# A decoder layer's output projection in seven block products, with its weight sums on GpSimd and their low parts through DRAM

## The chip, the core and the metric

The kernel runs on one core of one Trainium2 chip. The metric is device time in microseconds (us) of one execution: 1641.2 us before the change, the median of 3 runs (1641.06 to 1641.68). A core has a matrix engine (PE, whose weight loads are shown as PEld), a vector engine (DVE), an activation engine (ACT), GpSimd (POOL) and SyncE (SP), which here only issues DMAs. Each engine takes its own instructions strictly in order; they wait for one another through semaphores.

## The reference, cut to what matters

```python
merged = (gates[:, :, 0] * (y_sb @ w_sb_out[l])
          + gates[:, :, 1] * (y_ml @ w_ml_out[l])
          + gates[:, :, 2] * (y_xa @ w_xa_out[l]))
x = x + merged @ w_o[l]

h = _rmsnorm(x, g_ffn[l])
u = _causal_dwconv(h @ w_up[l], ff_conv_w[l], ff_conv_b[l])
```

The sequence has 1024 rows and the model 1024 columns, all in float32. Three mixers (stick-breaking attention, mLSTM, cross-attention) make y_sb, y_ml and y_xa of 512 columns each. Their projections are gated and added (`merged`), and one 1024 x 1024 product with `w_o` writes to the residual stream. An RMS norm and a gated MLP follow.

## The kernel before

Everything lies transposed, columns on the 128 partitions and the 1024 sequence rows along the free axis, in tiles of 128 x 1024 floats (a page, 512 KB). h = 1 and h = 0 name the two halves of 512 rows. To keep float32 precision PE multiplies in three passes: each operand is split into a rounded part `hi` and a rest `lo` (`split`, L128: a copy on ACT at L129, a subtraction on DVE at L130), and `mm3` (L141) does hi by hi, hi by lo, lo by hi, three matmuls of 128 x 512 (L142 to L144) for one block of 128 x 128 weights. In PSUM there are eight banks of 128 x 512: two each under the tags pj, pv, tr and z.

Three stages matter here.

**The branch stage** (L1067 to L1088). For each of three branches b and each of eight column blocks n, PE makes two banks (h = 1, 0) of four `mm3`, 24 matmuls in all, from the branch's weights `w_br` and the split pages `ys` of y. DVE takes each bank with the gate (`scalar_tensor_tensor`, L1083 and L1085) and adds it to `merged[n]` (L1086). The gates, the weights and the y pages come from DRAM by SP: gates through tag U (L1057), weights through `raw` (L135), the four y pages of branches 1 and 2 through `px` (L1064, two buffers), from where they are split into `h`. The y pages of branch 0 are split into `pg`. So b = 2 needs four pages through the two `px` buffers.

**The output projection** (L1091 to L1149). `merged` is split into `m_hi` and `m_lo`, half by half, beside the end of the branch stage. Then for h = 1 and h = 0 and each of eight column blocks d, `proj` loads and splits a page of `w_o` and runs eight `mm3`: 2 x 8 x 8 x 3 = 384 matmuls. `ev` (L1114) takes the bank into the residual x1 (L1119), stores x1 to DRAM (L1120), and squares and adds it for the norm (L1123 to L1126). During h = 0 the norm of h = 1 is applied and the first MLP operands are made (`h2_upper`, L1100), and `diff` is begun (L1130).

**The MLP's entry** (L1176 to L1211). The MLP already works by seven block products in place of eight (`seven`, L694, Winograd's form of Strassen). Its operands need sums of the four quarters of the normed x1, made and split on DVE and ACT from L1188 on while PE begins the first products.

The order on each engine is made by a scheduler when the kernel is built, by priorities and by its own guess of durations; on the chip it is fixed. A tile pool gives out a tag's buffers in turn: who wants a buffer waits until its last user is done.

## Time and profile before

| | before |
|---|---|
| median of 3 runs | 1641.2 us |
| the profiled execution | 1641.45 us |
| its span, first to last instruction | 1639.7 us |
| PE busy, share of the span | 99% |
| DVE, ACT, POOL busy | 74%, 50%, 6% |
| granted TensorE clock | 1.000 |
| DMA, mean over the span | 130 GB/s |

The span is 1.75 us shorter than the profiled execution's time. A row of a timeline gives start (us from the span's start), duration, engine, line, operation, output and inputs, and in brackets how long the engine had been idle and who ended that. Matmuls overlap, so a matmul's duration of 0.39 us is longer than the distance from one to the next. A group of a source view gives durations in ns as least, median and greatest.

### The profile page before, as it was taken

Reading aid. Unit: us, or ns where it says so; the run is one execution under the profiler, and the core shown is the slowest. Engines: PE = TensorE matmul, PEld = TensorE weight load, DVE = VectorE, ACT = ScalarE, POOL = GpSimd, SP = SyncE. Lnnn points to the kernel's source line nnn. Section 1 sums busy time; section 2 is a strip of 40 time slices with the busy share of each in tenths; the row PEclk is TensorE's granted clock in tenths of the full one; section 3 lists DMA queues with packets and bytes.
Section 4 is the critical chain, followed back from the end, with each engine's and each line's share of the span. In section 5 each row is a group of like instructions: output and inputs, shape, how many; then the busy total and the mean of one; then the engine's idle time right before and its main releaser. Section 6 shows DMA issues by size and latency. Waiting matters only on the chain.

```text
span 1639.7 us, 21300 instructions
## 1 busy us (share of the span) xinstructions
PE 1623.8 (99%) x8007; PEld 1330.6 (81%) x8007; DVE 1205.9 (74%) x1672; ACT 822.3 (50%) x1269; POOL 95.9 (6%) x164
## 2 busy tenths in 40 slices
PE   8999999999999999999999999999999999999999
PEld 4878888888888888888888888788888888888887
DVE  5658888759764776776657658997777777799764
ACT  4557777545554444666412334655555545543431
POOL 1022222020000010100000000000000000000000
PEclk9999999999999999999999999999999999999999
DMA  8420111324324665434844453322222221576131
GB/s 298 155 66 21 39 40 65 140 94 152 129 99 154 191 193 156 137 115 153 313 151 129 155 187 107 123 97 71 78 78 100 92 78 52 177 310 244 46 135 71
DMA packets 97426, 212.70 MB, mean 130 GB/s; under 512 B 13416, under 2 KB 37288, under 8 KB 97324
## 3 DMA queue, kind: packets, MB, share of 16 engines
q1 hardware_dynamic: 97324, 211.35, 38.1%
q8 instruction: 63, 1.03, 0.3%
q14 instruction: 39, 0.32, 0.1%
HBM read 156.71 MB, written 54.61 MB: 129 GB/s over the span
## 4 chain that ended last, share of the span: by engine, by line
PE 93%; DVE 3%; DMA 2%; ACT 1%; issue 1%; SPq 0%; POOLq 0%; POOL 0%; ACTq 0%; DVEq 0%
PE ps_pj L142 15%; PE ps_pj L143 15%; PE ps_pj L144 15%; PE ps_pv L142 6%; PE ps_pv L144 6%; PE ps_pv L143 6%; PE ps_tr L144 4%; PE ps_tr L142 4%; PE ps_tr L143 4%; PE ps_z L142 3%; PE ps_z L143 3%; PE ps_z L144 3%; PE ps_pv L444 2%; PE ps_tr L424 2%; PE ps_z L399 1%; PE ps_z L398 1%
## 5 line engine op out<-in xcount | busy, mean ns | idle before, releaser
L143 PE MATMUL ps_pj<-h,whi 128*128 128x512 f32 x624 | 244.1, 391 | 1.0 <-DVE h L130 1.0
L129 ACT ACTIVATE whi<-raw 128x512 fp32r<-128x512 f32 (+1 forms) x111 | 93.1, 839 | 180.8 <-PE ps_pj L143 74.8
L142 PE MATMUL ps_pj<-h,whi 128*128 128x512 f32 x416 | 165.9, 399 | 0.2 <-ACT h L129 0.2
L142 PE MATMUL ps_pj<-pg,whi 128*128 128x512 f32 x396 | 154.4, 390 | 0.0
L144 PE MATMUL ps_pj<-pg,wlo 128*128 128x512 f32 x376 | 146.5, 390 | 0.0
L143 PEld LDWEIGHTS ps_pj<-h,whi 128*128 128x128 f32 x624 | 117.3, 188 | 25.1 <-DVE h L130 1.9
L144 PE MATMUL ps_pj<-h,wlo 128*128 128x512 f32 x328 | 128.2, 391 | 0.1
L835 DVE SCALAR_TENSOR_TENSOR y<-U,vec,y 128x1023 f32<-128x1023 f32 x88 | 112.4, 1278 | 7.6 <-ACT y L833 7.5
L412 DVE TENSOR_TENSOR_SCAN U<-U 128x512 f32<-128x512 f32 (+3 forms) x96 | 92.7, 1007 | 22.1 <-POOL U L407 20.5
L142 PEld LDWEIGHTS ps_pj<-h,whi 128*128 128x128 f32 x416 | 78.2, 188 | 16.3 <-ACT h L129 1.1
L142 PEld LDWEIGHTS ps_pj<-pg,whi 128*128 128x128 f32 x396 | 74.3, 188 | 15.2
L144 PEld LDWEIGHTS ps_pj<-pg,wlo 128*128 128x128 f32 x376 | 70.6, 188 | 15.0 <-DVE wlo L130 0.3
L130 DVE TENSOR_TENSOR wlo<-raw,whi 128x1024 fp32r<-128x1024 f32 x54 | 65.9, 1221 | 18.3 <-ACT whi L129 18.3
L143 PE MATMUL ps_pj<-pg,whi 128*128 128x512 f32 x188 | 73.4, 390 | 0.0
L144 PEld LDWEIGHTS ps_pj<-h,wlo 128*128 128x128 f32 x328 | 61.6, 188 | 13.8 <-DVE wlo L130 0.6
L129 ACT ACTIVATE whi<-pg 128x512 fp32r<-128x512 f32 (+1 forms) x46 | 35.3, 769 | 61.8 <-PE ps_pv L143 18.2
L833 ACT ACTIVATE y<-U,vec 128x1024 f32<-128x1024 f32 x44 | 54.6, 1241 | 17.4 <-DVE U L726 16.9
L144 PE MATMUL ps_pj<-h,whi 128*128 128x512 f32 x160 | 62.3, 390 | 0.0
L144 PE MATMUL ps_pv<-pg,wlo 128*128 128x512 f32 x150 | 58.4, 389 | 0.0
L130 DVE TENSOR_TENSOR wlo<-raw,wlo 128x512 fp32r<-128x512 f32 x55 | 37.8, 687 | 26.5 <-ACT wlo L129 26.2
L401 ACT ACTIVATE U<-ps_z 128x1024 f32<-128x1024 f32 (+3 forms) x48 | 39.1, 814 | 31.9 <-PE ps_z L399 24.0
L144 PE MATMUL ps_tr<-pg,wlo 128*128 128x512 f32 x140 | 54.5, 389 | 0.0
(463 smaller groups left out, 4310.4 us busy)
## 6 DMA issues: line engine op xcount, KB each, us to landing
raw<-in_w_t_dram SPq DMA_DIRECT2D x29, 512.0 KB
gate_d<-U SPq DMA_DIRECT2D x24, 512.0 KB
U<-gate_d SPq DMA_DIRECT2D x22, 512.0 KB
act_d<-y SPq DMA_DIRECT2D x22, 512.0 KB
pg<-in_w_t_dram SPq DMA_DIRECT2D x21, 512.0 KB
raw<-in_w_dn_dram SPq DMA_DIRECT2D x18, 512.0 KB
raw<-in_w_o_dram SPq DMA_DIRECT2D x16, 512.0 KB
h<-act_d SPq DMA_DIRECT2D x14, 512.0 KB
```

The costliest lines, as they stand in the source:

```text
L129: nc.scalar.activation(hi, src, AF.Copy)
L130: (eng or nc.vector).tensor_sub(lo, src, hi.bitcast(F32))
L142: nc.tensor.matmul(out, lh, rh, start=start, stop=False, skip_group_check=more)
L143: nc.tensor.matmul(out, lh, rl, start=False, stop=False, skip_group_check=more)
L144: nc.tensor.matmul(out, ll, rh, start=False, stop=stop, skip_group_check=more)
L398: nc.tensor.matmul(z[:, a, :w], qs[a][:, ts(rb)], ks[a][:, c], start=True, stop=False)
L401: nc.scalar.activation(f[:, :, 1:w + 1], z[:, :, :w], AF.Sigmoid, scale=-0.125)
L412: nc.vector.tensor_tensor_scan(f[:, a, 1:w + 1], f[:, a, 1:w + 1], f[:, a, 1:w + 1], 1.0 if o == 0 else f[:, a, 0:1], op0=ALU.mult, op1=AL ...
L424: nc.tensor.transpose(pt[:, a, ts(j)], g[:, a, ts(j)], ident)
L444: nc.tensor.matmul(pv[64 * a:64 * a + 64, ts(rb % 4)], sbv[s // 2][:, s % 2, (2 * p + a) * 64:(2 * p + a + 1) * 64], wt[a][:, ts(j)], star ...
L833: nc.scalar.activation(out, u, AF.Identity, bias=bias, scale=taps[0])
L835: nc.vector.scalar_tensor_tensor(out[:, :S - s], u[:, s:], taps[s], out[:, :S - s], op0=ALU.mult, op1=ALU.add)
```

## The change

It concerns the three stages above. `merged` now lies as quarters (two halves of the rows, two halves of the columns), and the output projection becomes seven block products, each of 4 column blocks by 4 inner blocks by 3 passes = 48 matmuls: 336 in place of 384. The seven products accumulate in two sets of four banks (L: pj and tr, R: pv and z). Three of them use plain quarters of `w_o`, loaded and split as before (`raw_w`). The other four use sums of quarters, S1 to S4, each of two pages. GpSimd makes these sums in the branch stage (`wo_sums`, one step of the generator behind each unit of branches 1 and 2), eight additions and subtractions of 128 x 1024. For each of the eight sum pages `spill` also makes the rounded part (on ACT) and the rest (on GpSimd), both in the two `px` buffers, and SP stores the rest to DRAM (`slo_d`). In the projection `sum_w` rounds the sum page again on ACT and fetches the rest from DRAM by a DMA that GpSimd issues.

In the branch stage the column blocks come in the order 0, 4, 1, 5, ... and each `w_br` load brings two blocks that lie apart. The x1 quarters are built up in place from the loaded x (`grow`): 32 reads of a bank by DVE in place of 16. The MLP's upper operands are made two blocks at a time (`upper`).

```diff
+    ORDER = (0, 4, 1, 5, 2, 6, 3, 7)
+    merged = [[[page() for _ in range(2)] for _ in range(2)] for _ in range(2)]
+    slo_d = dtile([4, 2, P, S], "slo_d")
...
+    def wo_load(q, i, j, tag):
+        t = T([P, S], tag)
+        n = 4 * i + 2 * j
+        nc.sync.dma_start(t.rearrange("p (n c) -> p n c", n=2), w_o[n:n + 2, :, hs(q)].rearrange("n p c -> p n c"))
+        return t
...
+    def spill(i, j):
+        hi, lo = T([P, S], "px", F32R), T([P, S], "px", F32R)
+        split(ws[i][j], hi, lo, nc.gpsimd)
+        nc.sync.dma_start(slo_d[i, j], lo.bitcast(F32))
+
+    def wo_sums(j):
+        a1, a2 = wo_load(0, 0, j, "pg"), wo_load(0, 1, j, "pg")
+        yield
+        nc.gpsimd.tensor_sub(a2, a1, a2)
+        ws[2][j] = a2
+        spill(2, j)
+        b2 = wo_load(1, 1, j, "pg")
+        yield
+        nc.gpsimd.tensor_sub(b2, b2, a2)
+        ws[1][j] = b2
+        spill(1, j)
...
     for i in range(3 * KT):
-        b, n = i // KT, i % KT
+        b, n = i // KT, ORDER[i % KT]
         if n == 0:
             ys = [branch(b, j) for j in range(4)]
...
+        if b:
+            next(beside, None)
+        if i == 3 * KT - 5:
+            first_operands(0)
+        if i >= 3 * KT - 2:
+            w1.append(wsplit(None, raw=wo_load(0, 0, len(w1), "raw")))
...
+    def part_product(banks, w, n, start):
+        for d in range(4):
+            hi, lo = w[d // 2]
+            for k in range(4):
+                c = slice((4 * (d % 2) + k) * P, (4 * (d % 2) + k + 1) * P)
+                mh, ml = m[n][k // 2]
+                mm3(banks[d], hi[:, c], lo[:, c], mh[:, hs(k % 2)], ml[:, hs(k % 2)], start and k == 0, k == 3, not start)
+            yield d
...
+    def sum_w(i, j):
+        t = [T([P, S], tag, F32R) for tag in ("whi", "wlo")]
+        nc.scalar.activation(t[0], ws[i][j], AF.Copy)
+        nc.gpsimd.dma_start(t[1], slo_d[i, j])
+        return t
...
+    for d in part_product(L, w6, "t1", False):
+        if d == 0:
+            r = rstd(acc[1], HALF, "z")
...
+        if d > 1:
+            upper(0, o1u, d - 2, dau)
+        grow(o2l, L, d)
+        squares(0, part(o2l, d))
+        if d % 2:
+            keep(o2l, 1, 0, d // 2)
+        grow(o1l, L, d)
...
+    for d in part_product(R, w7, "bl", True):
...
+        grow(o1l, R, d)
+        squares(0, part(o1l, d))
+        nc.vector.scalar_tensor_tensor(part(diff, d), part(o1l, d), minus[:, d:d + 1], part(o2l, d), op0=ALU.mult,
+                                       op1=ALU.add)
+        if d % 2:
+            keep(o1l, 0, 0, d // 2)
+            upper(2, o2u, d // 2, dbu)
```

Three places show what the scheduler made of it. The first is SP's queue in the branch stage. Before, the loads of branch 2's four y pages (px from y_d) stand among the gate (U) and weight (raw) loads of the start of branch 1:

```order
L1064 DMA px_7681<-y_d 128x1024
L1057 DMA U_7345<-gate_d 128x1024
L135 DMA raw_7471<-in_w_br_dram 128x1024
L1064 DMA px_7687<-y_d 128x1024
L1057 DMA U_7375<-gate_d 128x1024
L1064 DMA px_7693<-y_d 128x1024
L1064 DMA px_7699<-y_d 128x1024
L1057 DMA U_7437<-gate_d 128x1024
```

In the changed kernel the same four loads, px_7746 to px_7764, stand behind the stores of all eight rests (slo_d); the last of these stores are:

```order
L1079 DMA slo_d<-px_7696 128x1024
L1125 DMA raw_7840<-in_w_br_dram 128x2x512
L1058 DMA U_7806<-gate_d 128x1024
L1079 DMA slo_d<-px_7736 128x1024
L1125 DMA raw_7916<-in_w_br_dram 128x2x512
L1058 DMA U_7838<-gate_d 128x1024
L1079 DMA slo_d<-px_7742 128x1024
L1065 DMA px_7746<-y_d 128x1024
L1065 DMA px_7752<-y_d 128x1024
L1058 DMA U_7876<-gate_d 128x1024
L1125 DMA raw_7986<-in_w_br_dram 128x2x512
L1065 DMA px_7758<-y_d 128x1024
```

The y pages of branch 2 moved from the start of branch 1 to behind the eighth store, and each store waits for GpSimd's subtraction that makes it; gate and weight loads stand between the stores.

The second place is GpSimd's queue behind the mixers. Before, its last instructions are small ones, the reciprocal roots of the norms (L150):

```order
L150 TENSOR_TENSOR sm_5895<-sm_5893,nhalf 128x8
L150 TENSOR_TENSOR sm_6220<-sm_6218,nhalf 128x8
L150 TENSOR_TENSOR sm_6537<-sm_6535,nhalf 128x8
L150 TENSOR_TENSOR sm_6847<-sm_6845,nhalf 128x8
L150 TENSOR_TENSOR sm_8430<-sm_8428,nhalf 128x4
```

Now sixteen operations of 128 x 1024 stand there, of which the first twelve are these (pg are weight pages and their sums; L130 with px is the subtraction that makes a rest):

```order
L1084 TENSOR_TENSOR pg_7442<-pg_7440,pg_7442 128x1024
L1089 TENSOR_TENSOR pg_7482<-pg_7482,pg_7442 128x1024
L130 TENSOR_TENSOR px_7478<-pg_7442,px_7477 128x1024
L1094 TENSOR_TENSOR pg_7440<-pg_7440,pg_7482 128x1024
L1097 TENSOR_TENSOR pg_7528<-pg_7528,pg_7482 128x1024
L130 TENSOR_TENSOR px_7524<-pg_7482,px_7523 128x1024
L1084 TENSOR_TENSOR pg_7614<-pg_7612,pg_7614 128x1024
L130 TENSOR_TENSOR px_7564<-pg_7440,px_7563 128x1024
L1089 TENSOR_TENSOR pg_7654<-pg_7654,pg_7614 128x1024
L1094 TENSOR_TENSOR pg_7612<-pg_7612,pg_7654 128x1024
L130 TENSOR_TENSOR px_7570<-pg_7528,px_7569 128x1024
L130 TENSOR_TENSOR px_7650<-pg_7614,px_7649 128x1024
```

Nothing is moved here; it is added. Two sums stand ahead of the first rest, two more ahead of the second, one ahead of the third, two ahead of the fourth; of the last four rests (the fifth is the last row) only the sixth has a sum ahead of it.

The third place is DVE's queue at the end of the projection. Before, for the column blocks d = 4 to 6 of h = 0 (L1119 takes a bank, L130 splits a weight page or an operand):

```order
L1102 SCALAR_TENSOR_TENSOR pg_8032<-U_8047,vec,ps_tr_8437 128x512 x2
L1102 SCALAR_TENSOR_TENSOR pg_8033<-U_8048,vec,ps_tr_8437 128x512
L1119 SCALAR_TENSOR_TENSOR px_8347<-ps_pj_8541,hf_8566 128x512
L1102 SCALAR_TENSOR_TENSOR pg_8033<-U_8048,vec,ps_tr_8437 128x512
L1130 SCALAR_TENSOR_TENSOR h_8042<-px_8347,vec,y_8345 128x512
L1126 TENSOR_TENSOR hf_8344<-hf_8344,hf_8566 128x512
L130 TENSOR_TENSOR h_8038<-pg_8032,h_8038 128x512
L130 TENSOR_TENSOR wlo_8624<-raw_8621,whi_8623 128x1024
L1119 SCALAR_TENSOR_TENSOR px_8347<-ps_pj_8583,hf_8608 128x512
L1130 SCALAR_TENSOR_TENSOR h_8042<-px_8347,vec,y_8345 128x512
```

Now, for the last part (L1186 takes a bank, L1268 makes two blocks of an upper operand, L1202 adds squares):

```order
L1202 TENSOR_TENSOR hf_8071<-hf_8071,hf_8606 128x512
L1186 SCALAR_TENSOR_TENSOR y_8491<-ps_pv_8611,y_8491 128x512
L1268 TENSOR_TENSOR pg_8489<-U_8315,raw_8558 128x1024
L1308 SCALAR_TENSOR_TENSOR h_8495<-y_8491,sm_8505,px_8173 128x512
L1186 SCALAR_TENSOR_TENSOR y_8491<-ps_pv_8612,y_8491 128x512
L1202 TENSOR_TENSOR hf_8071<-hf_8071,hf_8643 128x512
L1308 SCALAR_TENSOR_TENSOR h_8495<-y_8491,sm_8505,px_8173 128x512
L130 TENSOR_TENSOR h_8502<-pg_8489,h_8501 128x1024
L1202 TENSOR_TENSOR hf_8071<-hf_8071,hf_8660 128x512
L130 TENSOR_TENSOR U_8680<-me_8631,U_8680 128x512
```

The split of a weight page has gone from this stretch, and more reads of banks and the operands' multiplications and splits of 128 x 1024 have come into it, while a column block now lasts 12 matmuls where it lasted 24.

More of the change, by code (lines that the diff above doesn't have):

```diff
@@ new lines, in both, with gain, operand @@
+    def both(op, t, rows):
+        v = t.rearrange("p (k r) -> p k r", k=2)
+        op(v, v, rows.unsqueeze(1).to_broadcast([P, 2, HALF]))
+    def gain(o, i):
+        for d in range(4):
+            nc.scalar.activation(part(o, d), part(o, d), AF.Copy, scale=col(C_GFFN + 4 * i + d))
+    L, R = four(LONG[::-1]), four(SHORT)
+    w2, w3, w4, w5, w6, w7 = ([None, None] for _ in range(6))
+    def operand(n, src):
+        for j in range(2):
+            m[n][j] = fine(src[j], "h")
+    o1u = out_tiles(0, 1, "U")
@@ new lines, in tile_hybrid_layer @@
+    operand("bu", bu)
+    operand("t3", al)
+    for d in part_product(L, w1, "au", True):
+        if d % 2 == 0:
+            w2[d // 2] = raw_w(1, 0, d // 2)
+        grow(o1u, L, d)
+    operand("t2", au)
+    o2l = out_tiles(1, 0, "px")
+    for d in part_product(R, w2, "bu", True):
+        if d % 2 == 0:
+            w3[d // 2] = sum_w(2, d // 2)
+        grow(o1u, R, d)
+    for j in range(2):
+        keep(o1u, 0, 1, j)
+        nc.vector.tensor_sub(bu[j], bu[j], au[j])
+    R = four(SHORT)
@@ L1153, in tile_hybrid_layer @@
+    x1p = o1l + o2l
     act_d = dtile([NF // 2, 2, P, S], "act_d")
@@ L1189, in tile_hybrid_layer @@
         for j in range(2):
-            for i in range(2):
-                nc.vector.tensor_mul(diff[j][:, hs(i)], diff[j][:, hs(i)], rows)
+            both(nc.vector.tensor_mul, diff[j], rows)
             nc.vector.tensor_add(full[j], full[j], diff[j])
```

180 lines of the change are left out of this document (115 added, 65 removed).

## The prediction

> **What bounds the kernel now.** I read the page first: which engine is busy all the time.
>
> ```profile
> span 1639.7 us, 21300 instructions
> PE 1623.8 (99%) x8007; PEld 1330.6 (81%) x8007; DVE 1205.9 (74%) x1672; ACT 822.3 (50%) x1269; POOL 95.9 (6%) x164
> ```
>
> PE is. Then the table of stages (busy us and instructions per engine, clock, DMA share, GB/s), cut at the starts of the branches, the projection and the MLP's entry, and PE's own waits between 783 and 1050 us (us in total, times, longest).
>
> ```profile
> 826.70:870.20 43.50, 43.50 (x193) 36.03 (x192) 26.01 (x35) 4.24 (x4) 0.00 (x0) 1.00 0.47 145
> 870.20:913.80 43.60, 43.60 (x194) 36.08 (x194) 34.58 (x50) 13.64 (x20) 0.00 (x0) 1.00 0.33 104
> 913.80:1001.50 87.70, 87.70 (x391) 72.40 (x390) 54.55 (x76) 33.30 (x46) 1.89 (x1) 1.00 0.58 190
> 1001.50:1050.00 48.50, 47.31 (x207) 37.55 (x206) 46.50 (x65) 25.77 (x38) 1.01 (x1) 1.00 0.20 68
> ```
>
> ```profile
> PE ps_pj L143 <- DVE h L130: 1.0, 2, 0.5
> PE ps_pj L142 <- ACT h L129: 0.2, 1, 0.2
> ```
>
> In branch 1 (826.7 to 870.2), branch 2 (to 913.8) and the projection (to 1001.5) PE never waits. At the entry it waits 1.2 us, and DVE is nearly as full as PE: 46.5 of 48.5 us. So a matmul less is time saved, as long as nothing new makes PE wait. GpSimd stands idle in branches 1 and 2.
>
> **Part 1, the matmuls.** Two rows of PE's timeline that stand 48 matmuls apart:
>
> ```profile
> 791.36 0.39 PE L142 MATMUL ps_pj<-pg,whi 128*128 128x512 f32 x1
> ...
> 802.24 0.39 PE L142 MATMUL ps_pj<-pg,whi 128*128 128x512 f32 x1
> ```
>
> 48 matmuls take 10.88 us, 0.227 us each. The projection goes from 384 to 336, so **-10.9 us**. That is the whole gain.
>
> **Part 2, the spills.** Branch 2 can't start before its first y page is loaded (px) and rounded. By the order of SP that load now stands behind the stores of all eight rests, and a rest needs the px buffer that the store before it has to empty. So there is a chain: store of one rest, GpSimd's subtraction for the next, its store, eight times over. I need its start, the store S and a GpSimd operation P.
>
> The start: the weight pages for the sums take the pg buffers of branch 0's y pages, free in its last bank.
>
> ```profile
> 826.49 0.39 PE L144 MATMUL ps_pj<-pg,wlo 128*128 128x512 f32 x1
> 826.72 0.39 PE L142 MATMUL ps_pj<-h,whi 128*128 128x512 f32 x1
> ```
>
> Branch 0's last matmul starts at 826.5, branch 1's first at 826.7, and branch 2's by 192 matmuls more at 870.2. A bank is 12 matmuls, 2.7 us, and its first three read the first pages, so these loads go out at about 825. For a page's way from DRAM I take SP's issues of px pages and ACT's start on them:
>
> ```profile
> 799.91 0.33 SPq L1064 DMA_DIRECT2D px<-y_d  x1
> 805.63 0.32 SPq L1064 DMA_DIRECT2D px<-y_d  x1
> 808.99 0.32 SPq L1064 DMA_DIRECT2D px<-y_d  x1
> ```
>
> ```profile
> 803.28 1.06 ACT L129 ACTIVATE h<-px 128x1024 fp32r<-128x1024 f32 x1 [3.46 <-DMA px<-y_d]
> 809.25 1.06 ACT L129 ACTIVATE h<-px 128x1024 fp32r<-128x1024 f32 x1 [1.54 <-DMA px<-y_d]
> 814.22 1.06 ACT L129 ACTIVATE h<-px 128x1024 fp32r<-128x1024 f32 x1 [3.91 <-DMA px<-y_d]
> ```
>
> 3.4 and 3.6 us, and 5.2 where others are under way. The first sum needs two pages, one behind the other: 825 + 5 = 830. A store of a whole page isn't in these rows; as the same bytes in the other direction I take S = 3.6, with 3.4 and 5.2 as ends.
>
> P has no row either. The nearest, in ns (least, median, greatest):
>
> ```profile
> L498 POOL TENSOR_TENSOR mw<-mw,mw x1: 453/453/453, 94.0 to 94.0; 32x128 f32<-32x128 f32 x1
> L880 POOL TENSOR_SCALAR_AFFINE_SELECT me<-me x8: 634/739/1079, 357.9 to 626.2; 128x512 f32<-128x512 f32 x8
> L407 POOL TENSOR_SCALAR_AFFINE_SELECT U<-U x64: 398/408/1387, 103.2 to 298.0; 128x256 f32<-128x256 f32 x64
> ```
>
> One input: 634 - 398 = 236 ns for 256 columns, so 0.92 a column over a fixed 0.16 us, and 1.1 us for 1024: the lower end. Two inputs: 453 ns for 128 columns; less 0.16 that is 2.3 ns a column, 2.5 us for 1024; scaled whole it is 3.6, the upper end. I take P = 2.3, a little under 2.5, since two inputs may well cost more of the fixed part. The Trainium skill, "GPSIMD Engine Reference", section "Elementwise — side-by-side cycle accounting", gives 4497 ns for a two-input addition of 2048 floats on GpSimd against 2293 on DVE; half of that, 2.25 us, is an estimate from that page, and by it the sum would be 0.7 us less. The same page's "Engine selection" speaks against this change: elementwise work belongs on VectorE.
>
> Now the chain, by GpSimd's order. Two sums and a rest: 3P = 6.9, so 836.9. Of the seven cycles that follow, two have two sums inside (4.6, more than S): 3P = 6.9 each. The other five are S + P = 5.9 each. 836.9 + 13.8 + 29.5 = 880.2.
>
> To this comes the meeting of DVE and GpSimd:
>
> ```profile
> 162.25 1.22 DVE L130 TENSOR_TENSOR wlo<-raw,whi 128x1024 fp32r<-128x1024 f32 x1
> ...
> 162.49 1.60 POOL L407 TENSOR_SCALAR_AFFINE_SELECT U<-U 128x256 f32<-128x256 f32 x2
> ```
>
> Two GpSimd operations beside a DVE subtraction of two SBUF tiles took 1.60 us together, where two medians are 0.82: 0.8 lost to one meeting. In branch 1 DVE has 16 additions of 0.69 and four splits of 1.22 of that kind, 16 of 43.5 us; about a third of the 14 operations on the chain meet one, at half of it on average (0.4): +2 us, 882.2. (The rule for this is a rival, below.)
>
> Then SP stores and issues the y page (0.35), it lands (3.6), ACT rounds it (1.06): 887.2 in place of 870.2, **+17.0 us**.
>
> **Part 3, the other y pages.** Before, they were loaded during branch 1. Now page 1 waits for the eighth store, 882.2 + 3.6 = 885.8, lands at 889.4, is rounded at 890.5, and its rest is made at 891.7:
>
> ```profile
> L130 DVE TENSOR_TENSOR h<-px,h x8: 1216/1224/1226, 798.7 to 821.4; 128x1024 fp32r<-128x1024 f32 x8
> ```
>
> Only then is its buffer free for page 3: 891.7 + 3.6 + 1.06 + 1.22 = 897.6. The first bank of branch 2 needs page 3's rest for its last two matmuls, so it ends at 898.1, against 887.2 + 2.7 = 889.9: **+8.2 us**. While PE waits in either part, DVE falls idle; there is no cover to lose. Queued behind the waiting stores on SP are gate and weight loads, and behind ACT's roundings for the spills, which wait for GpSimd's sums, ACT's roundings of the weight pages. DVE waits for both and PE for DVE; but the chain doesn't depend on them, so they only make PE wait earlier for part of what it would wait for at branch 2.
>
> **Part 4, the projection itself.** The rests come back by GpSimd's own DMAs, which the profile before doesn't show. A weight page serves 24 matmuls, 5.4 us, and there are two buffers, so a load that takes under 5.4 us (the rows above have 3.4 to 5.2) is hidden: 0, up to +1 for each of eight loads if it takes 6.4. The Trainium skill, "DMA: Bandwidth & Descriptors", section "Anatomy of one DMA — SWDGE (gpsimd) path", would put it at 2.0 us plus bytes over 436 GB/s, an estimate of 3.2 us for a page; by that too the term is 0. The splits of `merged` were hidden beside the branch stage and are, as seven operands, spread over the parts (DVE has 33 us free there); the first of them are made before part 1. `rstd` stands behind the first bank of part 6 and needs the last squares of part 5, some 2 us of ACT and DVE behind a bank of 2.7 us with ACT's weight rounding in between: **+1 us**.
>
> **Part 5, DVE at the end.** DVE's work in the last two parts against the same stretch before:
>
> ```profile
> 979.70:1001.50 21.80, 21.80 (x98) 18.05 (x97) 18.29 (x27) 9.64 (x15) 0.00 (x0) 1.00 0.65 205
> ```
>
> ```profile
> L1119 DVE SCALAR_TENSOR_TENSOR U<-ps_pj,hf x8: 690/690/693, 919.4 to 957.5; 128x512 f32<-128x512 f32 x8
> L1126 DVE TENSOR_TENSOR hf<-hf,hf x14: 682/684/687, 926.9 to 1004.7; 128x512 f32<-128x512 f32 x14
> L1130 DVE SCALAR_TENSOR_TENSOR h<-px,vec,y x4: 743/749/753, 987.7 to 1004.0; 128x512 f32<-128x512 f32 x4
> L170 DVE TENSOR_SCALAR hf<-ident,sm x8: 277/279/285, 971.4 to 1008.6; 128x128 f32<-128x128 f32 x8
> ```
>
> Now 12 reads of banks (8.3), 7 additions of squares (4.8), four upper operands multiplied and split (8 x 1.22 = 9.8), four `diff` (3.0), four 128 x 128 (1.1) and two half splits (1.4): 28.4 us in two parts of 10.9, 21.8. 6.6 us pass on to the entry, where DVE has 2.0 free. Fewer, longer operations there save 0.5, and waits among these operations eat about as much: **+5 us**, from 0 to 8.
>
> **Sum**: -10.9 + 17.0 + 8.2 + 1 + 5 = +20.3. The profiled execution, 1641.45 with 1.75 outside its span, would become 1661.8; it lies 0.25 over the median of 1641.2, so I predict **1661.5 us**.
>
> **The rivals.**
>
> *GpSimd is quick* (P = 1.1, the one-input pace). Every cycle is then S + P = 4.7: 830 + 3.3 + 32.9 = 866.2, plus 1 for meetings and 5.0 for the page: 872.2, +2.0. The sum is -10.9 + 2.0 + 8.2 + 1 + 5 = +5.3, 1646.5 us. Against it: the two-input row is twice the one-input slope.
>
> *GpSimd is slow, or the rests come back late.* With P = 2.9, between 2.5 and the upper end, part 2 grows by 14 x 0.6 = 8.4: 1670. With 3.6 by 18: 1680. Loads of 6.4 us add 8.
>
> *DVE and GpSimd shut each other out.* If each holds the other off for a whole instruction, GpSimd's 16 x 2.3 = 36.8 us and DVE's two-input work of 16 to 20 us share the 57 us from 830 to 887 and just fill them. A few cycles then wait for a whole DVE operation: some 3 to 5 us in place of my 2, 1664. The Trainium skill, "SBUF — State Buffer", section "Who interferes with whom", states just this: a DVE instruction with two SBUF inputs and a GpSimd instruction that reads SBUF exclude each other. The 1.60 us row agrees.
>
> *Hidden (the other side).* The spills stay ahead of branch 2, so neither part 2 nor 3 is paid: -10.9 + 1 + 5 = -4.9, 1636.5 us. It decides where the last rest is made 13 us before 870.2, at 857: 27 us for eight rests, 3.4 each. With S alone at 3.4 GpSimd would have to take nothing. For it speaks only that a store may land sooner than a load.
>
> *It does not do what it says*: the count of matmuls in the program falls by 48, so this is out.
>
> **How the numbers follow.** Forecast with its near bounds, 1654 to 1670: 0.52. DVE and GpSimd shutting each other out, 1660 to 1670: 0.12. GpSimd slow or late rests, above 1670: 0.16. GpSimd quick, 1645 to 1654: 0.12. Hidden or nearly so: 0.08, of which 0.05 below 1638 and 0.03 about the old time. A measurement of this kernel can tell about 0.2%, 3.3 us, from no change. The range of 8 in 10 takes in the quick and some of the slow case: 1645 to 1677. Faster 0.05, same 0.03, slower 0.92.
>
> **What would show it.** Right: PE waits between 826 and 900, in two lumps, one in branch 1 behind a bank that DVE can't take (it waits for a late weight page), one at branch 2's start behind ACT's rounding of px, 25 us together; GpSimd's L130 rows about 2.3 us each, 6 us apart; the table of stages with DVE full at the entry and PE idle 6 us there. Wrong: GpSimd's 128 x 1024 operations near 1.1 us; branch 2 starting less than 5 us behind branch 1's last matmul; stores that land in under 3 us; PE waits inside the seven parts for `wlo`.

## The result, and the profile after

The changed kernel takes 1669.4 us (median of 4 runs, 1666.3 to 1670.6) against 1641.2 before, a ratio of 1.0168 with a 95% interval of 1.0151 to 1.0186: slower by 28.2 us, where 20.3 were forecast (the time lies inside the range of 1645 to 1677). The profiled execution took 1668.9, with a span of 1667.2. Its page:

```profile
span 1667.2 us, 21227 instructions
PE 1627.1 (98%) x7959; PEld 1326.9 (80%) x7959; DVE 1234.3 (74%) x1673; ACT 838.5 (50%) x1278; POOL 140.7 (8%) x188
```

The 48 matmuls are gone (8007 to 7959), and yet PE is busy 3.3 us longer. So not only waits were added. The table of stages, cut at the first matmul of branch 1, branch 2, the projection and what follows its 336 matmuls, shows why (the columns are those of before):

```profile
825.67:889.51 63.84, 46.87 (x193) 37.16 (x191) 44.49 (x39) 14.48 (x14) 41.34 (x16) 0.90 0.72 243
889.51:939.42 49.91, 48.93 (x193) 37.12 (x193) 34.52 (x43) 9.42 (x9) 0.00 (x0) 0.92 0.52 162
939.42:1020.91 81.49, 79.84 (x347) 65.40 (x346) 62.02 (x81) 44.99 (x57) 5.62 (x9) 0.98 0.43 130
1020.91:1069.40 48.49, 42.60 (x168) 32.50 (x167) 45.22 (x60) 22.47 (x32) 1.42 (x1) 0.93 0.22 73
```

Branch 1 takes 63.8 us (the wait for branch 2's first page counted in) and branch 2 49.9, where each took 43.5, and the granted clock, 1.00 in each stage before, is below 1 in all four. PE's waits from 826 to 1050 us:

```profile
PE ps_pj L142 <- DVE U L1138: 11.7, 3, 10.3
PE ps_pj L142 <- ACT h L129: 7.5, 4, 5.6
PE ps_z L158 <- DVE hf L1202: 1.6, 1, 1.6
PE ps_pj L144 <- DVE U L130: 1.5, 1, 1.5
PE ps_pj L143 <- DVE h L130: 1.3, 1, 1.3
PE ps_tr L158 <- DVE hf L1202: 0.6, 1, 0.6
PE ps_pv L143 <- DVE h L130: 0.4, 1, 0.4
```

They are the two lumps that were forecast, 10.3 us in branch 1 behind a bank and 5.6 at branch 2's start behind ACT's rounding of a y page, and then small ones at `rstd` and the entry. But the lumps were to make 25 us together. In the two branches PE is idle for 17.0 and 1.0 us (length less busy in the table); the other 8.8 of the 26.7 us lost there are busy time, 3.4 and 5.4 more than the 43.5 of before. What the forecast lacks is half clock: windows like these three, behind the branches (length, PE busy and its instructions, ..., the clock before the last two columns):

```profile
999.65:1003.06 3.41, 3.41 (x10) 2.65 (x9) 1.42 (x5) 1.33 (x2) 1.04 (x1) 0.50 0.01 3
1030.37:1033.78 3.41, 3.41 (x10) 2.63 (x9) 3.08 (x10) 0.58 (x2) 1.42 (x1) 0.50 0.47 191
1044.02:1047.43 3.41, 3.41 (x10) 2.63 (x9) 3.41 (x5) 0.00 (x0) 0.00 (x0) 0.50 0.00 0
```

In each PE is busy all the time, at half the clock: some eight matmuls 0.427 us apart in place of fifteen at 0.227, 1.6 us lost each. Six more such windows lie in the branches, behind the two lumps: from 859.70 to 869.94 and from 887.01 to 897.25. The start of branch 2 shows what they look like, with 14 recorded matmuls in 7.7 us:

```profile
889.51:897.25 7.74, 7.47 (x14) 3.84 (x14) 3.55 (x3) 2.11 (x2) 0.00 (x0) 0.50 0.82 283
```

No run prices these six by themselves. Branch 2's start (889.5) comes behind the first three, and the rest of its last y page (899.6, see Part 3 below) behind the other three. Neither is made by PE, so by the trace most of the slow matmuls stood in time that PE would have waited anyway.

One small table serves all that follows: the time of PE's first matmul in branch 1, branch 2 and the projection, and the span, of each profiled execution (us). "Branches" is the time from the first to the third, less the 87.0 of before; "rest" is the time from the third to the span's end, less the 725.9 of before. The full gain from 48 fewer matmuls would be a rest of -10.9 (e2 and e11 have the old projection). One profiled execution can lie some way from its kernel's median: e5's is 3.8 us above it, e1's 2.2 above, e12's 3.5 below. So differences of 2 or 3 us between rows mean little by themselves.

| kernel | branch 1 | branch 2 | projection | span | branches | rest |
|---|---|---|---|---|---|---|
| before | 826.7 | 870.2 | 913.8 | 1639.7 | 0 | 0 |
| after | 825.7 | 889.5 | 939.4 | 1667.2 | +26.7 | +1.9 |
| e1, no spill | 828.7 | 878.4 | 921.9 | 1645.8 | +6.2 | -2.0 |
| e2, sums and spills alone | 825.4 | 888.5 | 938.4 | 1664.4 | +26.0 | +0.1 |
| e3, y buffers, GpSimd's queue | 827.9 | 895.0 | 938.5 | 1666.3 | +23.6 | +1.9 |
| e4, y buffers, SP's queue | 827.3 | 885.6 | 929.1 | 1657.1 | +14.8 | +2.1 |
| e5, hi by GpSimd too | 828.7 | 886.2 | 939.8 | 1665.9 | +24.1 | +0.2 |
| e6, sums by DVE | 827.6 | 873.6 | 917.2 | 1641.7 | +2.5 | -1.4 |
| e7, additions later | 825.6 | 890.5 | 941.4 | 1669.0 | +28.7 | +1.7 |
| e9, filled waits | 825.8 | 889.9 | 939.7 | 1663.1 | +26.9 | -2.5 |
| e10, no additions of squares | 826.6 | 890.7 | 940.4 | 1658.3 | +26.7 | -8.0 |
| e11, spill without stores | 825.6 | 894.8 | 938.4 | 1664.3 | +25.7 | 0.0 |
| e12, sums by DVE, chain first | 826.5 | 871.5 | 915.0 | 1639.1 | +1.4 | -1.8 |

### The profile page after: what moved, and what is told of

The parts are those of the page before. It is cut to its first block, busy times and chain, and to the rows that moved or that the text cites. A ratio compares the mean times of both kernels' runs of the same rounds, so it can differ in the third digit from the quotient of the medians.

```text
span 1667.2 us, 21227 instructions
## 1 busy us (share of the span) xinstructions
PE 1627.1 (98%) x7959; PEld 1326.9 (80%) x7959; DVE 1234.3 (74%) x1673; ACT 838.5 (50%) x1278; POOL 140.7 (8%) x188
## 4 chain that ended last, share of the span: by engine, by line
PE 89%; DMA 4%; DVE 3%; ACT 2%; POOL 1%; issue 1%; SPq 0%; ACTq 0%; POOLq 0%; DVEq 0%
PE ps_pj L142 13%; PE ps_pj L143 12%; PE ps_pj L144 12%; PE ps_pv L144 5%; PE ps_pv L143 5%; PE ps_pv L142 5%; PE ps_tr L144 4%; PE ps_tr L142 4%; PE ps_tr L143 4%; PE ps_z L142 4%; PE ps_z L144 4%; PE ps_z L143 4%; PE ps_pv L440 2%; PE ps_tr L420 2%; PE ps_z L395 1%; PE ps_z L394 1%
## 5 line engine op out<-in xcount | busy, mean ns | idle before, releaser
L143 PE MATMUL ps_pj<-h,whi 128*128 128x512 f32 x520 | 206.1, 396 | 2.2 <-DVE h L130 2.0
L142 PE MATMUL ps_pj<-h,whi 128*128 128x512 f32 x440 | 179.0, 408 | 19.2 <-DVE U L1138 11.7
L129 ACT ACTIVATE whi<-raw 128x512 fp32r<-128x512 f32 (+1 forms) x101 | 82.5, 817 | 154.7 <-PE ps_pj L143 55.1
L144 PE MATMUL ps_pj<-h,wlo 128*128 128x512 f32 x352 | 139.1, 396 | 0.1
L143 PEld LDWEIGHTS ps_pj<-h,whi 128*128 128x128 f32 x520 | 99.0, 190 | 25.1 <-DVE h L130 5.9
L142 PEld LDWEIGHTS ps_pj<-h,whi 128*128 128x128 f32 x440 | 83.9, 191 | 40.1 <-DVE U L1138 13.3
L142 PE MATMUL ps_pj<-pg,whi 128*128 128x512 f32 x268 | 104.5, 390 | 0.0
L144 PE MATMUL ps_pj<-pg,wlo 128*128 128x512 f32 x248 | 96.7, 390 | 0.0
L130 DVE TENSOR_TENSOR wlo<-raw,whi 128x1024 fp32r<-128x1024 f32 x44 | 54.4, 1235 | 29.4 <-ACT whi L129 29.3
L143 PE MATMUL ps_pv<-h,whi 128*128 128x512 f32 x190 | 73.9, 389 | 0.0
L143 PE MATMUL ps_pj<-pg,whi 128*128 128x512 f32 x188 | 73.4, 390 | 0.0
L144 PE MATMUL ps_pj<-h,whi 128*128 128x512 f32 x160 | 62.6, 391 | 0.0
L144 PE MATMUL ps_pv<-h,wlo 128*128 128x512 f32 x152 | 59.5, 392 | 0.0
L142 PE MATMUL ps_pv<-h,whi 128*128 128x512 f32 x150 | 58.5, 390 | 0.4 <-DVE U L722 0.4
L142 PEld LDWEIGHTS ps_pj<-pg,whi 128*128 128x128 f32 x268 | 50.3, 188 | 10.2
L130 DVE TENSOR_TENSOR wlo<-raw,wlo 128x512 fp32r<-128x512 f32 x55 | 37.8, 687 | 26.6 <-ACT wlo L129 26.2
L397 ACT ACTIVATE U<-ps_z 128x1024 f32<-128x1024 f32 (+3 forms) x48 | 39.1, 814 | 32.0 <-PE ps_z L395 24.1
```

What stands on the lines that cost most here:

```text
L129: nc.scalar.activation(hi, src, AF.Copy)
L130: (eng or nc.vector).tensor_sub(lo, src, hi.bitcast(F32))
L142: nc.tensor.matmul(out, lh, rh, start=start, stop=False, skip_group_check=more)
L143: nc.tensor.matmul(out, lh, rl, start=False, stop=False, skip_group_check=more)
L144: nc.tensor.matmul(out, ll, rh, start=False, stop=stop, skip_group_check=more)
L397: nc.scalar.activation(f[:, :, 1:w + 1], z[:, :, :w], AF.Sigmoid, scale=-0.125)
```

## The experiments

My theory after the result: the branch stage loses 26.7 us because the spills' chain (rest, store, px buffer) holds up what stands behind it, and the end loses 12.8 (from -10.9 to +1.9), part to DVE's load and part to the clock. The rivals: GpSimd's arithmetic itself, and a chain of single steps at the entry. Each ratio below is to 12 to 15 executions of the kernel before, run beside the changed one (medians 1641.0 to 1642.0).

### Take the spills out, and put them in alone (e1, e2)

e1, in the changed kernel:

```diff
     def spill(i, j):
-        hi, lo = T([P, S], "px", F32R), T([P, S], "px", F32R)
-        split(ws[i][j], hi, lo, nc.gpsimd)
-        nc.sync.dma_start(slo_d[i, j], lo.bitcast(F32))
+        return
...
     def sum_w(i, j):
-        t = [T([P, S], tag, F32R) for tag in ("whi", "wlo")]
-        nc.scalar.activation(t[0], ws[i][j], AF.Copy)
-        nc.gpsimd.dma_start(t[1], slo_d[i, j])
-        return t
+        return wsplit(None, raw=ws[i][j])
```

> The changed kernel without the spills: GpSimd still makes the eight weight sums in the branch stage, but their rests are made by DVE in the projection, where the pages are used, and nothing goes through DRAM or px. Chain theory (the px buffers, the stores and SP's order hold back branch 2, which the profile after prices at 26.8 us of PE's waits and slow matmuls between 784 and 939 us): these go, what is left is -10.9 for the matmuls, +12.5 for the end of the projection and the entry, and 2 to 5 for the DVE subtractions that come back where DVE is full; 1645 to 1648 us, no PE wait over 2 us between 800 and 900. Rival, GpSimd's work itself (it shuts DVE out at their shared access to SBUF): the eight sums stay, so a good part of the loss in the branch stage stays too; above 1652, with PE waiting there for DVE.

e2, in the kernel before: `wo_load`, `spill`, `wo_sums` as in the changed kernel, and in the loop

```diff
+        if b:
+            next(beside, None)
```

> The kernel before, with the weight sums and spills of the changed kernel added in branches 1 and 2, and nothing else changed: the old projection, no matmul less; what is spilled is never read. Chain theory: the whole loss of the branch stage comes with the spills, +24 to +28 us, 1665 to 1669, with branch 2's first matmul about 17 to 20 us behind the kernel before. Rival, the loss comes from the new order of the banks, the earlier operand splits or the new weight tiles of the branch stage rather than from the spills: under 1655.

e1 took 1645.3 us (ratio 1.0022, 1.0012 to 1.0032), e2 1667.5 (1.0164, 1.0149 to 1.0179). The sums and spills, put in alone, make all of the loss in the branches (+26.0 of +26.7), and without the spills 6.2 are left. e1 lies in its band by two misses that cancel: the branches were to lose nothing and lost 6.2, and the rest, forecast at +3.6 to +6.6, came at -2.0. What the 6.2 are e1's trace shows. GpSimd's sums, and DVE beside and after them:

```profile
844.04 3.38 POOL L1094 TENSOR_TENSOR pg<-pg,pg 128x1024 f32<-128x1024 f32 x1
847.38 2.85 POOL L1081 TENSOR_TENSOR pg<-pg,pg 128x1024 f32<-128x1024 f32 x1
850.30 2.74 POOL L1086 TENSOR_TENSOR pg<-pg,pg 128x1024 f32<-128x1024 f32 x1
```

```profile
841.75 3.41 DVE L130 TENSOR_TENSOR wlo<-raw,whi 128x1024 fp32r<-128x1024 f32 x1
845.09 0.67 DVE L1135 SCALAR_TENSOR_TENSOR U<-U,ps_pj 128x512 f32<-128x512 f32 x1
845.79 2.17 DVE L1136 TENSOR_TENSOR pg<-pg,U 128x512 f32<-128x512 f32 x1
...
860.34 0.69 DVE L1136 TENSOR_TENSOR pg<-pg,U 128x512 f32<-128x512 f32 x1
```

The same addition takes 2.17 us beside GpSimd and 0.69 after its last sum, the subtraction 3.41 in place of 1.22; the operation that reads a bank (`ps_pj`) takes 0.67 either way. Over the stretch of GpSimd's sums DVE's operations of this kind take 10.6 us longer than without them. PE waits once for DVE there, 3.1 us, and a half-clock stretch follows. The Trainium skill, "SBUF — State Buffer", section "Who interferes with whom", has a DVE instruction with two SBUF inputs and a GpSimd instruction that reads SBUF exclude each other; these rows agree.

### Free the buffers and SP (e3, e4)

The spills go to the y buffers, idle in these branches; in e3 GpSimd's own queue stores them, in e4 SP as before:

```diff
-        hi, lo = T([P, S], "px", F32R), T([P, S], "px", F32R)
+        hi, lo = T([P, S], "y", F32R), T([P, S], "y", F32R)
         split(ws[i][j], hi, lo, nc.gpsimd)
-        nc.sync.dma_start(slo_d[i, j], lo.bitcast(F32))
+        nc.gpsimd.dma_start(slo_d[i, j], lo.bitcast(F32))
```

> The changed kernel with the spills in the two y buffers, which stand idle in branches 1 and 2, and their stores issued by GpSimd's own queue, so that neither px nor SP knows of them. GpSimd's sums and rests and the bytes stored are the same. Chain theory: the loss of the branch stage goes, 1641 to 1645 us. Rival, GpSimd's work and DRAM traffic themselves: still 1650 and more. If the branch stage costs nothing here, the end of the projection and the entry should still show the +12.5 us that they have in the changed kernel.

> As the one with the y buffers, but the stores stay on SP, where gate and weight loads queue behind them; only the px buffers and the place of the y page loads in SP's order (now ahead of the stores) differ from the changed kernel. If the px buffers are the whole cause: 1641 to 1645, as with GpSimd's queue. If SP's order matters by itself (gate and weight loads held behind stores that wait for a rest): the PE wait of some 10 us in branch 1 stays and only branch 2's start and its later pages get better, about 1653 to 1658.

e3 took 1667.1 us (1.0156, 1.0141 to 1.0171), e4 1657.6 (1.0094, 1.0077 to 1.0111). So px and the stores on SP were not the whole cause: with both freed in e3, 23.6 us stay. e3's waits of ACT and of DVE from 826 to 900 us:

```profile
ACT y L129 <- POOL y L130: 41.3, 7, 7.8
ACT y L129 <- POOL pg L1084: 8.3, 1, 8.3
```

```profile
DVE wlo L130 <- ACT whi L129: 22.5, 4, 11.4
```

ACT works in order too. Its rounding of each spilled sum waits for GpSimd (41.3 us in seven waits), and the rounding of the branch weights stands behind it; DVE waits for those, 22.5 us. In the changed kernel ACT waits 34.9 us at the same place. e4 came out in its band, but ACT waits in it as well, so it doesn't price SP's order by itself.

### Take ACT out too (e5)

```diff
-        split(ws[i][j], hi, lo, nc.gpsimd)
-        nc.sync.dma_start(slo_d[i, j], lo.bitcast(F32))
+        nc.gpsimd.tensor_copy(hi, ws[i][j])
+        nc.gpsimd.tensor_sub(lo, ws[i][j], hi.bitcast(F32))
+        nc.gpsimd.dma_start(slo_d[i, j], lo.bitcast(F32))
```

> The changed kernel with the spills in the y buffers, stores by GpSimd's queue, and the rounding of each spilled sum (hi) by GpSimd too. So px, SP and now ACT have nothing to do with the chain, which goes on inside GpSimd alone. Theory of the three in-order queues (the chain of rest, store, buffer holds up whatever stands behind one of its members in a queue: y pages behind px and SP, and the rounding of branch weights behind ACT's rounding of the spilled sums; with px and SP freed, ACT alone still held 27 us): now the branch stage loses only what GpSimd's arithmetic costs DVE, 4 to 6 us as without spills; 1641.2 - 10.9 + 12.5 + 5 = 1648, 1645 to 1650. Rival, GpSimd's arithmetic itself (16 operations with two SBUF inputs and 8 copies hold DVE): PE's waits for DVE in the branch stage stay at 10 us and more, 1655 to 1665.

1663.8 us (1.0133, 1.0117 to 1.0149; the profiled execution, 1667.6, is the slowest of the four): the rival's band. DVE's additions, 0.69 us alone, now take

```profile
849.15 5.86 DVE L1140 TENSOR_TENSOR pg<-pg,U 128x512 f32<-128x512 f32 x1
854.93 0.68 DVE L1139 SCALAR_TENSOR_TENSOR U<-U,ps_pj 128x512 f32<-128x512 f32 x1
855.64 3.66 DVE L1140 TENSOR_TENSOR pg<-pg,U 128x512 f32<-128x512 f32 x1
```

since GpSimd has an operation ready whenever one ends; PE waits 10.8 us for DVE up to 900 us. And a third queue showed itself: SP's next load into a y buffer stood waiting for the last rest, with gate and weight loads behind it.

```profile
SPq L1180 <- POOL y L1079: 19.5, 1, 19.5
```

PE's last wait in the branches, 6.5 us at 921, is for a page behind this one. So what e5 has lost is part arithmetic, part a new hold of my own making.

### Leave out the stores (e11)

```diff
         split(ws[i][j], hi, lo, nc.gpsimd)
-        nc.sync.dma_start(slo_d[i, j], lo.bitcast(F32))
```

> The kernel before with the sums and spills (1667.5 us), less the eight stores to DRAM: a px buffer is free as soon as the rest that used it is made. So the chain has GpSimd's operations and ACT's roundings in it, but no S. Theory of the sum S + P for five of the cycles: without S each is P and ACT's rounding and the hand-overs, some 4 us in place of 5.9, the last rest is made about 7 to 10 us earlier and branch 2 starts as much earlier: 1658 to 1661. Rival, GpSimd's own 16 operations fill the time whether the stores are there or not: 1665 to 1668.

1666.7 us (1.0154, 1.0139 to 1.0170), with e2 at 1667.5. The last rest came some 8 us earlier, as by S + P, at 874.3 in place of 882.7 in e2 (and 883.7 in the changed kernel):

```profile
868.46 2.33 POOL L130 TENSOR_TENSOR px<-pg,px 128x1024 fp32r<-128x1024 f32 x1
871.96 2.34 POOL L130 TENSOR_TENSOR px<-pg,px 128x1024 fp32r<-128x1024 f32 x1 [1.17 <-ACT px L129]
```

and it was worth 0.8 us. In ACT's order a weight page of branch 1 stands behind these roundings:

```profile
870.83 1.06 ACT L129 ACTIVATE px<-pg 128x1024 fp32r<-128x1024 f32 x1 [3.56 <-POOL px L130]
871.79 1.04 ACT L129 ACTIVATE whi<-raw 128x1024 fp32r<-128x1024 f32 x1
```

so branch 1 itself is late: PE waits 20.1 us in it, in three waits, and not at all at branch 2's start. Both readings of the chain miss: its length was right, but it isn't the only thing that ends last. (The loads of branch 2's y pages still stood on SP behind px here, so the run doesn't isolate ACT's order either.)

### The sums by DVE (e6)

e1 with `nc.vector` in place of `nc.gpsimd` in `wo_sums`, and one more step between a load and its use.

> No GpSimd and no spill: as the kernel without spills (1645.3), but the eight weight sums are made by DVE, spread over branches 1 and 2. Theory of the shared access: without spills, DVE's additions of 128x512 took 2.17 us beside GpSimd's sums and 0.69 after them, and its 128x1024 subtractions 3.4 beside them, and PE waited 3.1 us for it; with DVE alone these waits go, although DVE gets 10 us more to do: 1639 to 1642 us. Rival, the loads of the weight pages and SP's order are what delays DVE there: 1645 as without spills, or more, since DVE has more to do.

1642.9 us (1.0003, 0.9994 to 1.0012), level with before. The groups of DVE's additions from 830 to 864 us, first of the changed kernel and then of e6 (busy us, mean ns):

```profile
L1139 DVE TENSOR_TENSOR pg<-pg,U 128x512 f32<-128x512 f32 x8 | 14.4, 1796 | 0.3
```

```profile
L1139 DVE TENSOR_TENSOR pg<-pg,U 128x512 f32<-128x512 f32 x12 | 8.3, 689 | 0.3
```

1796 ns against 689. DVE has eight more operations of 1.22 us and yet keeps up: the branches lose 2.5 us in place of 6.2. What GpSimd took off DVE (9.8 us of sums) it took back by shutting it out (the 10.6 us of e1). The two edits differ in one thing more, the extra step between load and use, and the two medians lie only 2.5 us apart, so the size is rough; the 0.69 us beside the 2.17 are not.

### The end of the projection: order, load and clock (e7, e10, e9)

e7 issues each addition of a square one square later, so that DVE need not wait for ACT's square (the last addition of each half stands ahead of its `rstd`, in `add_last`):

```diff
         nc.scalar.activation(t, x, AF.Square)
-        nc.vector.tensor_add(acc[h], acc[h], t)
+        add_last(h)
+        owed[h] = t
...
+            add_last(1)
             r = rstd(acc[1], HALF, "z")
```

> The changed kernel, with each DVE addition of squares issued one square later, so that DVE does not stand waiting for ACT's square in its own order (6.2 us of DVE idle time in the last parts of the projection and the entry). Nothing else. Theory that DVE is behind at the entry and PE waits for it there: DVE comes 4 to 6 us earlier, PE's waits between 990 and 1050 us (7.5 us) shrink, and with them some of the three stretches of half clock (about 1.6 us each): 1661 to 1666 against 1669. Rival, DVE's waits there are slack (what PE waits for comes from elsewhere): 1668 to 1670.

1669.9 us (1.0170, 1.0155 to 1.0185): the rival's band. But it doesn't show that those waits were slack, since most of them stayed. From 990 to 1050 us DVE waits 4.5 us for ACT's squares in place of 6.2, and PE waits for the last addition at both `rstd`, 1.8 and 1.9 us in place of 1.6 and 0.6:

```profile
DVE hf L1209 <- ACT hf L1201: 4.5, 3, 3.0
PE ps_tr L158 <- DVE hf L1209: 1.9, 1, 1.9
PE ps_z L158 <- DVE hf L1209: 1.8, 1, 1.8
```

e10 leaves the additions out, so that each scale of the norm is made of the first square alone:

```diff
         nc.scalar.activation(t, x, AF.Square)
-        nc.vector.tensor_add(acc[h], acc[h], t)
```

> The changed kernel without the fourteen DVE additions that sum up the squares (the two scales of the normalisation are then made of one square of eight): DVE gets 14 x 0.6 us less to do, eight of these additions in the last two parts and the entry, where it is full. Everything else, ACT's squares too, is the same. Theory that the end of the projection and the entry are set by DVE's amount of work: about 5 us of PE's waits there go, and a stretch of half clock with them: 1661 to 1665. Rival, a chain of single steps (last bank, square, rstd, rows, operands) sets the entry, and only the one addition in it counts: 1667 to 1669.

1660.1 us (1.0111, 1.0098 to 1.0125), 9.3 less than the changed kernel; its rest is -8.0 against +1.9. From 990 to 1050 us PE waits once:

```profile
PE ps_tr L168 <- DVE hf L166: 0.6, 1, 0.6
```

and the clock there is 1.00. The waits go, and the half clock that followed them; it gave more than the 5 that I had for it. Two causes are taken out here at once: 14 x 0.6 = 8.4 us of DVE's work, and the chain of last bank, square and addition that `rstd` stood behind. The run can't tell them apart. e9 asks what the half clock alone is worth, by matmuls that do nothing, six ahead of `rstd` and five in the entry:

```diff
+        for _ in range(fill[0] if fill else 0):
+            nc.tensor.matmul(pc, *fill[1:], start=True, stop=True)
         for t in range(nt):
             nc.tensor.matmul(pc[:, t:t + 1], acc[:, ts(t)], ones[:, :1], start=True, stop=True)
...
```

> The changed kernel with eleven matmuls that do nothing useful, put where PE waits: six ahead of the first rstd of the projection (into the bank that rstd then overwrites) and five at the MLP's entry, between the first two matmuls that use the operand t2 (into the bank that the next product overwrites). They lie in waits of 1.6 and 1.3 us and keep PE busy there; the rest of the kernel is the same. Theory that each stretch of half clock is paid in full: two of the three such stretches (those that begin at 999.7 and 1044.0 us) go, -3.2 us, about 1666. Theory that PE is held by DVE at the entry anyway: the first stretch was made good by shorter waits further on, and only the second is worth its 1.6 us: about 1668. Rival, the clock is not what costs: 1669 or more by the length of the fillers that don't fit (up to 2.5).

1666.2 us (1.0149, 1.0135 to 1.0162), 3.2 less than the changed kernel by the medians, though PE has eleven matmuls more to do. The two intervals overlap, and four executions of each are few, so the time saved is only roughly known; that the half clock went is plain. The stretch from 990 to 1050 us, first of the changed kernel (clock 0.91), then of e9 (1.00):

```profile
990.00:1050.00 60.00, 53.17 (x211) 41.23 (x210) 47.75 (x71) 28.29 (x40) 4.10 (x5) 0.91 0.41 127
```

```profile
990.00:1050.00 60.00, 55.45 (x241) 43.31 (x240) 50.23 (x74) 31.09 (x46) 4.10 (x5) 1.00 0.40 127
```

The third stretch, which I had not filled, went too, as the waits before it fell differently.

### How short a wait halves the clock (e8)

In the kernel before, four waits in the MLP:

```diff
+        if gap:
+            s = small(8)
+            nc.scalar.activation(s, L[:, :8], AF.Square)
+            for _ in range(gap):
+                s0, s = s, small(8)
+                nc.gpsimd.tensor_tensor(s, s0, nhalf, op=ALU.pow)
+            nc.tensor.matmul(p2[:, :1], ident, s[:, :1], start=True, stop=True)
         prod(p2, qring(b1), x["bu"])
...
+        return seven(w_up[f], w_up[NF + f], fx, done, early if f == 0 else None, {3: 1, 5: 2, 7: 3, 9: 5}.get(f, 0))
```

> The kernel before, with four waits of PE put into the MLP, about 100 us apart, where its clock is at full speed: ahead of a product, PE waits for a short chain of ACT and 1, 2, 3 and 5 small GpSimd operations, perhaps 2, 3, 4.5 and 7 us; a product's bank gets one extra column that is overwritten. Theory that short waits bring half clock: behind each of the four, the shortest too, there is at least one stretch of 3.41 us at half clock, in which eight matmuls take 0.427 us in place of 0.227, so that each costs its own length and 1.6 us more. Rival, short waits are harmless by themselves and the half clock at the entry comes from a series of waits: no half clock behind the first one or two. The Trainium skill, TensorE: Matmul & The Clock Gate, section HAM oscillation, gives the abstract rule that only idle gaps over about 3.4 us matter; by that the first two would be harmless.

1669.6 us (1.0167, 1.0150 to 1.0184). PE waited 1.9, 3.1, 4.9 and 8.0 us. The window of the first wait and the one behind it, then the two over which the second wait lies:

```profile
1063.81:1067.22 3.41, 1.55 (x9) 1.13 (x8) 3.41 (x4) 1.79 (x3) 1.94 (x1) 1.00 0.88 280
1067.22:1070.63 3.41, 3.41 (x10) 2.64 (x9) 1.33 (x2) 0.00 (x0) 0.00 (x0) 0.50 0.02 6
1104.77:1108.18 3.41, 1.56 (x7) 0.95 (x6) 0.83 (x3) 1.18 (x3) 2.12 (x2) 1.00 0.68 243
1108.18:1111.59 3.41, 2.20 (x11) 1.88 (x12) 1.36 (x2) 0.00 (x0) 1.16 (x1) 1.00 0.23 75
```

The 1.9 us cost a stretch of half clock and the 3.1 us none. Neither theory has that. (The four waits sum to 17.8 us of the 27.9 lost; there are six such windows in all.) All such stretches of one execution begin a whole number of 3.413 us apart (here 1067.22, 1152.56 and 1196.93: 25 and 13 of them; after the change 999.65, 1030.37 and 1044.02: 9 and 4), so there is a fixed grid, and the second wait lies astride one of its borders. The Trainium skill, "TensorE: Matmul & The Clock Gate", section "Part 1: The HAM clock gate", describes such a free-running window of 3413 ns; that agrees. Its abstract rule in "HAM oscillation", that there be no idle gaps over some 3.4 us, does not: 1.9 us were enough, and 1.6 with eight one-column matmuls at `rstd`.

### A try for a better kernel (e12)

e6, with the last squares, `rstd` and `spread` moved ahead of DVE's other work:

```diff
-        grow(o1l, R, d)
-        squares(0, part(o1l, d))
+        with tc.high_priority(offset=300):
+            grow(o1l, R, d)
+            squares(0, part(o1l, d))
...
-    r = rstd(acc[0], HALF)
+    with tc.high_priority(offset=300):
+        r = rstd(acc[0], HALF)
     next(first[0])
-    rows = spread(r, 4)
+    with tc.high_priority(offset=300):
+        rows = spread(r, 4)
```

> A try for a version that beats both: the weight sums by DVE, without GpSimd and without spills (1642.9 us, level with the kernel before), and the last squares, rstd and rows moved ahead of other work of DVE, which stood before them by up to 2 us. Theory that a chain of single steps sets the entry: 1 to 3 us less, 1640 to 1642, level with the kernel before or just under it. Rival, DVE's amount of work sets the entry: 1642 to 1644.

1644.3 us (1.0014, 1.0006 to 1.0023; its runs spread from 1640.8 to 1646.3, and the profiled one is among the fastest): not better than e6, and a little slower than before. The chain, moved ahead, didn't get shorter for PE: its wait at the last `rstd` is 2.7 us in the profiled execution, where it was 1.1 in e6. This order only moved the waits; that DVE's amount of work is what counts fits it, but isn't shown. No version here beats the kernel before.

## Why the prediction was right or wrong, point by point

**Part 1** holds: 48 matmuls less, 0.227 us each.

**Part 2** forecast a last rest at 882.2 and branch 2 at 887.2; they came at 883.7 and 889.5. P = 2.3 was the right value: GpSimd's two-input operations take 2.34 to 2.41 us alone and up to 3.36 beside DVE, and the stores landed 3.0 to 3.7 us after their issue (S = 3.6). Two cycles of the changed kernel, with the store issued between them:

```profile
875.85 2.39 POOL L130 TENSOR_TENSOR px<-pg,px 128x1024 fp32r<-128x1024 f32 x1 [3.75 <-DMA slo_d<-px]
881.28 2.40 POOL L130 TENSOR_TENSOR px<-pg,px 128x1024 fp32r<-128x1024 f32 x1 [3.04 <-DMA slo_d<-px]
```

```profile
878.27 0.32 SPq L1079 DMA_DIRECT2D slo_d<-px  x1
```

What failed there is a sentence beside the sum: that what is queued behind ACT's roundings "only" makes PE wait earlier for what it would wait for anyway. In e3, with the y buffers and the stores off SP, and in e11, without the stores, the branches still lose 23.6 and 25.7 us, behind ACT's roundings that wait for GpSimd. The sum came out because in the changed kernel the two lie over one another; that is luck.

**Part 3** had +8.2 behind branch 2's start; the branches lost 26.7 in all, 19.3 + 1.0 up to branch 2's start (which came 19.3 late though branch 1 began 1.0 early) and 6.4 behind it. Parts 2 and 3 together, 25.2 forecast, are right to 1.5. The path of Part 3 is there too: page 3's rest, forecast at 897.6, is made at 899.6, later by about what the chain before it is late:

```profile
897.32 1.06 ACT L129 ACTIVATE h<-px 128x1024 fp32r<-128x1024 f32 x1 [1.22 <-DMA px<-y_d]
898.41 1.23 DVE L130 TENSOR_TENSOR h<-px,h 128x1024 fp32r<-128x1024 f32 x1 [1.05 <-ACT h L129]
```

That PE's waits would make the whole 25 us was wrong, as said above: PE stood idle for 18.0 us, and the rest is matmuls that ran slowly.

**Part 4**: the rests came back in time, 4.7 us from issue to landing in the median, under the 5.4 that a weight page serves; no wait for `wlo` stands among PE's waits inside the parts. The 1 us for `rstd` was 1.6.

**Part 5 and the clock** hold the miss. Part 5 had DVE full in the last two parts, with 28.4 us of work for 21.8. In these parts, 27.0 us long, DVE was busy for 18.3 (the third column of busy times):

```profile
993.90:1020.91 27.01, 25.36 (x107) 20.27 (x106) 18.29 (x29) 17.18 (x25) 2.68 (x4) 0.94 0.46 143
```

The rest of the time it waited, 4.7 us of it for ACT's squares, and more of its work than forecast came only at the entry. So the step "28.4 us of work in 21.8" failed, and that PE's waits came out near the 6 is luck in part. The rest was forecast at -10.9 + 1 + 5 = -4.9 and came at +1.9. PE's waits from 990 to 1050 sum to 6.8 (the list above, with 1.4 of the 7.5 for ACT), 5.6 more than the 1.2 of before: the 6 of Parts 4 and 5. The three half-clock stretches add 4.8, and 2.4 are left over, 0.7 of them waits between 1050 and 1070. So the step that the sum didn't have at all is the clock: a wait of PE was priced at its own length. e8 shows half clock behind waits in a kernel that has nothing else of this change, and e9's lower time (3.2 us, with overlapping intervals) agrees with the price.

**The rivals.** DVE and GpSimd shutting each other out is real (e1, e5, e6), but little of it shows in the changed kernel's chain, which ended 1.5 us later than forecast. GpSimd quick, GpSimd slow and hidden are out by P and branch 2's start.

**What stays open:** how much of the branches' loss each queue would cost alone; each edit that freed one showed the next, and no run has the spills with all of them free. At the end of the projection it is open whether DVE's amount of work or the chain through the two `rstd` sets PE's waits. At the first `rstd` it was the chain, since DVE had itself just waited 2.9 us there for ACT's square. For the later ones no run separates the two.

## What to carry to other kernels

A value that one engine makes and another must wait for holds up everything behind the waiting instruction, on every queue that has a member of the chain: list them all (here SP, ACT and the buffer's next user) before pricing one. GpSimd's work is not free help for DVE: here eight sums on it cost DVE about as much as making them itself. And a wait of PE that leaves it idle for half of a 3.4 us window can cost up to 1.6 us more than its length, where matmuls stand ready to fill the next window.

## What the runs showed of the hardware

Half clock comes in windows of 3.413 us, and the window before decides. In the fourteen traces of this case, behind the first 60 us, every window at full clock in which PE was busy for 1.55 us or less was followed by half clock. From 1.56 to 1.77 us both happened: behind 1.56 (e8), 1.60 (e5) and 1.77 (the changed kernel) the clock stayed full, behind 1.69 (e4) and 1.75 (e7) it fell. So the border is not sharp by the profile's busy time. Above it the clock fell only behind windows in which one-column matmuls made a part of the busy time, as behind 2.43 us in the changed kernel, 1.05 of them such matmuls; it looks as if these don't count, but no run tests it. In a window that is itself at half clock busy time means less: the one from 890.42 of the changed kernel had 3.35 us of it, with seven matmuls, and half clock went on. Three windows of the changed kernel, the first with full clock behind it, the others with half:

```profile
1020.13:1023.54 3.41, 1.90 (x9) 1.26 (x8) 3.41 (x6) 1.41 (x3) 0.00 (x0) 1.00 0.41 154
1026.96:1030.37 3.41, 2.43 (x14) 1.64 (x13) 3.41 (x6) 1.14 (x2) 0.00 (x0) 1.00 1.02 291
1040.61:1044.02 3.41, 1.41 (x5) 0.97 (x6) 3.41 (x4) 2.66 (x3) 0.00 (x0) 1.00 0.00 0
```

A one-input GpSimd copy of 128 x 1024 took 1.05 us in e5 (its first 1.38), less than half of the two-input operation.
